# A hybrid decoder layer in split fp32: head products in runs of matmuls of one shape, activation rows at one byte remainder, block products pass by pass

## The chip, the cores and the metric

One core of one Trainium2 chip runs the whole layer as one program. The metric is the device time of an execution in microseconds; three executions of the kernel before gave 2039.51 to 2040.22, median 2040.07. TensorE (PE) multiplies, VectorE (DVE), ScalarE (ACT) and GpSimd (POOL) do the rest; SyncE (SP) and POOL issue the DMAs.

## The reference, cut to what matters

```python
h = concat([meta (16 rows), x (512 rows)])            # L = 528, D = 2048
p = rmsnorm(h, g_mix) @ w_in                          # q k v | b c u, 1024 columns each
q, k = rmsnorm per head of 128;  o_attn = stick_breaking_attention(q, k, v)   # 8 heads
o_conv = b * causal_dwconv3(c * u)
h = h + concat([rmsnorm(o_attn), rmsnorm(o_conv)]) @ w_out
n2 = rmsnorm(h, g_ffn)
h = h + (silu(n2 @ w_gate) * (n2 @ w_up)) @ w_down    # 5632 wide
return h[16:]
```

## The kernel before

Everything is kept transposed: channels on the 128 partitions, the 528 tokens on the free axis. The input x stands as 16 tiles of 128 channels (`nh0` to `nh15`), scaled by `g_mix`, each split into a rounded part `nh` and a remainder `nl` in the matmul type fp32r. A weight tile is split the same way into `hi` and `lo` in a ring `s_buf`: ACT casts `hi` (line 188), DVE subtracts for `lo` (line 189), `prepare` adds weight quarters where a Strassen product needs them (line 201). Each product is then three matmuls for each 128 x 128 weight block: `hi*ah`, `hi*al`, `lo*ah`. Weights come over SP's queue into `w_buf`.

The work runs in these stages, times from the profile: the eight heads and the first two channel blocks of the convolution (0 to 414 us), the Strassen pairs of the convolution (414 to 596), the output projection `po` (596 to 772), gate and up (772 to 1612), and down (to the end).

In the first stage `product_steps` takes one loaded weight piece of `m` blocks and goes block by block. `parts` says which columns of x go to which bank of PSUM. For k, v, c and u these are two parts, because one matmul writes at most one bank:

```python
product([(pk[:, 0, :H], 0, H), (pk[:, 1, :H], H, L)], n_hl)      # H = 264: two parts of 264
product([(pq[:, 0, :], META, L)], n_hl)                          # q: one part of 512
for j in range(m):
    for ps, a, b in parts: pe.matmul(ps, wh, ah[:, a:b], ...)    # L280
    for ps, a, b in parts: pe.matmul(ps, wh, al[:, a:b], ...)    # L282
    for ps, a, b in parts: pe.matmul(ps, wl, ah[:, a:b], ...)    # L284
    k += 1; tick()
```

So a k product is 16 blocks of six matmuls of 264 columns, whose moving operand alternates between the front and the back of a row and between `nh` and `nl`. A row of x is a tile of its own of 528 x 4 = 2112 bytes, that is 8 x 256 + 64, so neighbouring tiles begin at different remainders modulo 256. `tick()` counts blocks and starts the attention's steps (`after(n, work)`) in between; a list scheduler of the framework then orders each engine's instructions by priority and its own costs.

From channel block 2 on, the convolution and all of gate, up and down are Strassen pairs: `pair_product` makes two output blocks from seven block products `block_product(ps, act, ...)` into three PSUM banks `y`, `z`, `x`. Each has eight weight blocks, and the order is block by block: `hi*act0` (L742), `hi*act1` (L743), `lo*act0` (L744). Between them ACT copies a bank aside into `sides` (L768, L770, L772) and DVE combines (L774, L778, L783). In the convolution the two halves of x are 260 columns each; the sums of halves and quarters (`blk`) are formed by `form_blocks` during the heads, stored in DRAM (`fc`) and loaded back by POOL (L701, L708). In gate, up and down the operands have 256 columns, and their tiles (`slots`, `pad`) are laid out so that each block begins at the same remainder modulo 256; in `po` a row is 512 columns, 2048 bytes.

## Time and profile before

| What | Value |
|---|---|
| median of three executions | 2040.07 us |
| the profiled execution, its time | 2039.67 us |
| its span in the profile | 2038.0 us |
| PE busy, share of the span | 2028.5 us, 100% |
| DVE, ACT, POOL busy | 1718.7, 1049.0, 379.9 us |
| granted TensorE clock | 1.00 throughout |

A matmul's record lasts longer than its turn (a 256-column one 275 ns), since matmuls are pipelined. What a matmul costs the stream is the distance from its start to the next one's start, so that is read from the rows in order of time. Such a row reads: start, length, engine, line, operation, out<-in, rows * columns of the weights, partitions x columns of the moving operand, count. L numbers are lines of the kernel before.

### The profile page before, as it was taken

What the parts mean: (1) busy time and instruction counts of PE and PEld (TensorE: products, weight loads), DVE (VectorE), ACT (ScalarE), POOL (GpSimd) and SP (SyncE); (2) the same over time, 40 slices, a digit from 0 to 9 for tenths busy, and PEclk for the clock granted to TensorE, in tenths of its full rate; (3) what the DMA queues carried; (4) which work ended last, traced back from release to release, by engine and by line L of the source; (5) the groups of instructions that cost most, each with busy time, mean ns of one, the idle gap of its engine ahead of it and who ended that gap; (6) DMA issues with size and microseconds to landing.
All of it is one profiled execution on the core that took longest, in us unless ns stands there. A gap on an engine that the chain in (4) does not pass through costs nothing.

```text
span 2038.0 us, 39734 instructions
## 1 busy us (share of the span) xinstructions
PE 2028.5 (100%) x16158; PEld 1964.8 (96%) x16158; DVE 1718.7 (84%) x2202; ACT 1049.0 (51%) x1517; POOL 379.9 (19%) x532
## 2 busy tenths in 40 slices
PE   9999999999999999999999999999999999999999
PEld 8999999999998889999999999999999999999999
DVE  8788878588877678998988988988989988888887
ACT  7666666344443435554554554555555544444443
POOL 0111111210015440101111111110110252222111
PEclk9999999999999999999999999999999999999999
DMA  6333344753365656556555555555555999989864
GB/s 231 111 119 124 124 136 130 253 150 104 104 212 181 187 175 231 155 169 174 159 165 158 159 161 161 158 161 158 163 160 155 278 312 310 243 236 262 228 154 89
DMA packets 161863, 361.70 MB, mean 177 GB/s; under 512 B 13584, under 2 KB 73488, under 8 KB 161680
## 3 DMA queue, kind: packets, MB, share of 16 engines
q1 hardware_dynamic: 79744, 229.51, 35.5%
q0 software_dynamic: 81936, 129.65, 24.2%
q8 instruction: 127, 2.08, 0.4%
q14 instruction: 56, 0.46, 0.1%
HBM read 278.50 MB, written 80.61 MB: 176 GB/s over the span
## 4 chain that ended last, share of the span: by engine, by line
PE 93%; DVE 3%; ACT 2%; issue 1%; DMA 1%; POOL 0%; DVEq 0%; POOLq 0%; ACTq 0%
PE x L742 13%; PE x L744 13%; PE x L743 13%; PE z L742 6%; PE z L743 6%; PE z L744 6%; PE y L742 3%; PE y L743 3%; PE y L744 3%; PE po L843 3%; PE po L845 3%; PE po L844 3%; PE pv L280 2%; PE pv L284 1%; PE pv L282 1%
## 5 line engine op out<-in xcount | busy, mean ns | idle before, releaser
L188 ACT CAST s_buf<-w_buf 128x1024 fp32r<-128x1024 f32 (+2 forms) x665 | 659.3, 991 | 764.7 <-PE x L743 341.1
L189 DVE TENSOR_TENSOR s_buf<-w_buf,s_buf 128x1024 fp32r<-128x1024 f32 (+2 forms) x665 | 767.2, 1154 | 174.4 <-ACT s_buf L188 174.1
L742 PE MATMUL x<-f,s_buf 128*128 128x256 f32 x1408 | 387.7, 275 | 0.6 <-ACT sides L772 0.5
L744 PE MATMUL x<-f,s_buf 128*128 128x256 f32 x1408 | 387.2, 275 | 0.0
L743 PE MATMUL x<-f,s_buf 128*128 128x256 f32 x1408 | 387.2, 275 | 0.0
L201 DVE TENSOR_TENSOR w_buf<-w_buf 128x1024 f32<-128x1024 f32 (+1 forms) x243 | 277.5, 1142 | 14.7 <-DMA w_buf<-w_in 10.4
L742 PEld LDWEIGHTS x<-f,s_buf 128*128 128x128 f32 x1408 | 264.3, 188 | 1.4 <-ACT sides L772 0.9
L743 PEld LDWEIGHTS x<-f,s_buf 128*128 128x128 f32 x1408 | 264.3, 188 | 0.0
L744 PEld LDWEIGHTS x<-f,s_buf 128*128 128x128 f32 x1408 | 264.3, 188 | 0.0
L1038 POOL DMA_DIRECT2D fd<-s x147 | 103.6, 921 | 705.0 <-DVE s L295 703.7
L742 PE MATMUL z<-f,s_buf 128*128 128x256 f32 x704 | 193.6, 275 | 0.0
L743 PE MATMUL z<-f,s_buf 128*128 128x256 f32 x704 | 193.6, 275 | 0.0
L744 PE MATMUL z<-f,s_buf 128*128 128x256 f32 x704 | 193.6, 275 | 0.0
L744 PE MATMUL x<-ring,s_buf 128*128 128x256 f32 x608 | 167.3, 275 | 1.0 <-DVE s_buf L189 1.0
L742 PE MATMUL x<-ring,s_buf 128*128 128x256 f32 x608 | 167.2, 275 | 0.0
L743 PE MATMUL x<-ring,s_buf 128*128 128x256 f32 x608 | 167.2, 275 | 0.0
L742 PEld LDWEIGHTS z<-f,s_buf 128*128 128x128 f32 x704 | 132.1, 188 | 0.0
L744 PEld LDWEIGHTS z<-f,s_buf 128*128 128x128 f32 x704 | 132.1, 188 | 0.0
L743 PEld LDWEIGHTS z<-f,s_buf 128*128 128x128 f32 x704 | 132.1, 188 | 0.0
L1108 POOL DMA_DIRECT2D out_T<-d x62 | 60.2, 1001 | 302.7 <-DVE d L1116 232.3
L744 PEld LDWEIGHTS x<-ring,s_buf 128*128 128x128 f32 x608 | 114.1, 188 | 1.2 <-DVE s_buf L189 1.2
L742 PEld LDWEIGHTS x<-ring,s_buf 128*128 128x128 f32 x608 | 114.1, 188 | 0.0
(379 smaller groups left out, 5252.3 us busy)
## 6 DMA issues: line engine op xcount, KB each, us to landing
w_buf<-w_gu SPq DMA_DIRECT2D x176, 512.0 KB, 3.4
w_buf<-w_in SPq DMA_DIRECT2D x92, 512.0 KB, 3.4
fd<-s POOLq DMA_DIRECT2D x147, 256.0 KB, 5.2
w_buf<-w_down SPq DMA_DIRECT2D x96, 384.0 KB, 4.9
ring<-fd POOLq DMA_DIRECT2D x42, 768.0 KB, 8.7
w_buf<-w_out SPq DMA_DIRECT2D x32, 512.0 KB, 3.6
out_T<-d POOLq DMA_DIRECT2D x62, 256.0 KB, 5.4
fc<-st SPq DMA_DIRECT2D x8, 1040.0 KB, 6.2
```

The source lines that it names most:

```text
L188: sc.copy(hi, src)
L189: in_turn(ve.tensor_tensor(lo, src, hi.bitcast(F32), ALU.subtract), turn)
L201: in_turn(ve.tensor_tensor(sums[name], a, b, ALU.add), turn)
L280: pe.matmul(ps, wh, ah[:, a:b], start=k == 0, stop=False)
L742: pe.matmul(p, hi[:, kk], act(0, k), start=start and j == k == 0, stop=False, skip_group_check=skip)
L743: pe.matmul(p, hi[:, kk], act(1, k), start=False, stop=False, skip_group_check=skip)
L744: pe.matmul(p, lo[:, kk], act(0, k), start=False, stop=k == n - 1, skip_group_check=skip)
L843: pe.matmul(ps, hi[:, kk], ah, start=k == order[0], stop=False)
L844: pe.matmul(ps, hi[:, kk], al, start=False, stop=False)
L845: pe.matmul(ps, lo[:, kk], ah, start=False, stop=k == order[-1])
L1038: gp.dma_start(fd[c][s][:, :, k], t[:, :, i])
L1108: gp.dma_start(two(out[j]), c, accum_op=ALU.add)
```

## The change

- Rows of x: `nh` and `nl` of one channel tile become the two rows of one tile `n` with a pitch of 2304 bytes (9 x 256), from byte 48. All rows then begin at one remainder modulo 256.
- Heads and first convolution products: the row is cut at 272 (16 meta tokens and 256), so into 272 and 256 columns, q into 256 and 256; the two parts stand side by side in PSUM across the bank border, so later readers see one row of 528. The loop takes all blocks of a weight piece for the first part, then all for the second: 24 matmuls of one shape, then 24 of the other. `tick()` comes with the last part only.
- Convolution pairs: halves of 272 columns that overlap by 16, for c and u; the b product takes 256 of them. `blk` is laid out with a pitch of 1152 bytes.
- `block_product`: all `hi*act0`, then all `hi*act1`, then all `lo*act0`, everywhere.
- In `pair_product` the copies and combinations get the highest priority; in the first part of down the second sums are written behind the pair.
- x for `form_blocks` is loaded by a step of its own, earlier and in four DMAs of 272 columns; the scratch for POOL's DMA descriptors is 8192 bytes instead of 16384.

```diff
-            for j in range(m):
+            for i, ((ps, a, b), j) in enumerate((part, j) for part in parts for j in range(m)):
                 wh, wl = hi[:, j * P : (j + 1) * P], lo[:, j * P : (j + 1) * P]
-                ah, al = acts[k]
-                for ps, a, b in parts:
-                    pe.matmul(ps, wh, ah[:, a:b], start=k == 0, stop=False)
-                for ps, a, b in parts:
-                    pe.matmul(ps, wh, al[:, a:b], start=False, stop=False)
-                for ps, a, b in parts:
-                    pe.matmul(ps, wl, ah[:, a:b], start=False, stop=k == last)
-                k += 1
-                tick()
+                ah, al = acts[k + j]
+                pe.matmul(ps, wh, ah[:, a:b], start=k + j == 0, stop=False)
+                pe.matmul(ps, wh, al[:, a:b], start=False, stop=False)
+                pe.matmul(ps, wl, ah[:, a:b], start=False, stop=k + j == last)
+                if i % len(parts) == len(parts) - 1:
+                    tick()
+            k += m
...
-    H = L // 2
+    H, ROW = META + T2, 2304 // 4
...
-        nh = npool.tile([P, L], F32R, tag=f"nh{k}", name=f"nh{k}")
-        nl = npool.tile([P, L], F32R, tag=f"nl{k}", name=f"nl{k}")
+        n = npool.tile([P, 2 * ROW], F32R, tag=f"n{k}", name=f"n{k}")
+        n_row = n.rearrange("p (a t) -> p a t", a=2)[:, :, 12 : 12 + 2 * H]
+        nh, nl = (n_row[:, i, :L] for i in range(2))
...
+    def row_of(ps, a=0):
+
+        flat = ps.rearrange("p a b -> p (a b)")[:, 512 - H + a :]
+        return flat[:, : L - a], [(flat[:, : H - a], a, H), (flat[:, H - a : L - a], H, L)]
...
-    C0, CH = 8, (L - 8) // 2
+    CH = H
...
+        blk_x[k] = x4 = stage.tile([P, 4, CH], F32, tag="x4", name=f"x4_{k}")
+        for i, kk in ((0, k), (2, k + 8)):
+            for m in range(2):
+                nc.sync.dma_start(x4[:, i + m], xT[kk][:, m * T2 : m * T2 + CH])
...
-            product([(pk[:, 0, :H], 0, H), (pk[:, 1, :H], H, L)], n_hl)
+            product(row_of(pk)[1], n_hl)
...
-            product([(pq[:, 0, :], META, L)], n_hl)
+            product(row_of(pq, META)[1], n_hl)
...
+        if h:
+            after(22, lambda h=h: load_x4(h - 1))
...
-                    gp.dma_start(blk[:, i, part], fc[:, n, part], max_dma_last_dim=4160)
+                    gp.dma_start(blk[:, i, :, part, :CH], fc[:, n, part])
...
-        for j in range(m):
-            p, skip = ps[:, j * w : (j + 1) * w], m > 1 or not start
-            for k in range(n):
-                kk = slice((j * n + k) * P, (j * n + k + 1) * P)
-                pe.matmul(p, hi[:, kk], act(0, k), start=start and j == k == 0, stop=False, skip_group_check=skip)
-                pe.matmul(p, hi[:, kk], act(1, k), start=False, stop=False, skip_group_check=skip)
-                pe.matmul(p, lo[:, kk], act(0, k), start=False, stop=k == n - 1, skip_group_check=skip)
+        for wt, part in ((hi, 0), (hi, 1), (lo, 0)):
+            for j in range(m):
+                p, skip = ps[:, j * w : (j + 1) * w], m > 1 or not start
+                for k in range(n):
+                    kk = slice((j * n + k) * P, (j * n + k + 1) * P)
+                    first = start and wt is hi and part == j == k == 0
+                    pe.matmul(p, wt[:, kk], act(part, k), start=first, stop=wt is lo and k == n - 1, skip_group_check=skip)
...
         block_product(x, acts[2], False, m)
-        sc.copy(u2, x)
+        with tc.high_priority(1 << 20):
+            sc.copy(u2, x)
...
-        gbs = pair(conv_acts)
+        gbs = pair([last_of(act) for act in conv_acts], T2)
...
-            (lambda: load_acts(1, 6)) if j == KT // 4 - 1 else None, lambda: second_sums(4 * j, c2, 2),
+            (lambda: load_acts(1, 6)) if j == KT // 4 - 1 else None,
         )
+        second_sums(4 * j, c2, 2)
...
-    nc = bacc.Bacc("TRN2", target_bir_lowering=False, num_devices=1)
+    nc = bacc.Bacc("TRN2", target_bir_lowering=False, num_devices=1, dynamic_dma_scratch_size=8192)
```

What this does to the order of instructions is shown at three places. The first is PE at the start of the k product of head 3. `pk` is its PSUM tile, `nh`, `nl` and `n` with their numbers are tiles of x, `s_buf` the split weights. Before:

```order
L280 MATMUL pk_1569<-nh_170,s_buf 128x264 x2
L282 MATMUL pk_1569<-nl_171,s_buf 128x264 x2
L284 MATMUL pk_1569<-nh_170,s_buf 128x264 x2
L280 MATMUL pk_1569<-nh_174,s_buf 128x264 x2
L282 MATMUL pk_1569<-nl_175,s_buf 128x264 x2
L284 MATMUL pk_1569<-nh_174,s_buf 128x264 x2
```

In the change, at the place in the same product where the first part ends and the second begins on PE:

```order
L282 MATMUL pk_1704<-n_248,s_buf 128x272
L283 MATMUL pk_1704<-n_248,s_buf 128x272
L284 MATMUL pk_1704<-n_248,s_buf 128x272
L282 MATMUL pk_1704<-n_251,s_buf 128x272
L283 MATMUL pk_1704<-n_251,s_buf 128x272
L284 MATMUL pk_1704<-n_251,s_buf 128x272
L282 MATMUL pk_1704<-n_170,s_buf 128x256
L283 MATMUL pk_1704<-n_170,s_buf 128x256
L284 MATMUL pk_1704<-n_170,s_buf 128x256
L282 MATMUL pk_1704<-n_173,s_buf 128x256
```

The pairs of equal matmuls on one x tile have gone; 24 of 272 columns stand ahead of 24 of 256.

The second place is PE at the start of down, where the pair with `x_17616` (after: `x_18105`) follows the one with `x_17401` (after: `x_17890`); `ring` and `first` are operand tiles. Before, the scheduler put three matmuls of the new pair into the last block of the old one:

```order
L742 MATMUL x_17401<-first_17365,s_buf 128x256
L742 MATMUL x_17616<-ring_7922,s_buf 128x256
L743 MATMUL x_17616<-ring_7922,s_buf 128x256
L744 MATMUL x_17616<-ring_7922,s_buf 128x256
L743 MATMUL x_17401<-first_17365,s_buf 128x256
```

And in the change, on the same engine:

```order
L767 MATMUL y_17888<-first_17851,s_buf 128x256 x24
L767 MATMUL x_17890<-first_17854,s_buf 128x256 x24
L767 MATMUL x_18105<-ring_8411,s_buf 128x256 x24
L767 MATMUL z_18104<-first_17839,s_buf 128x256 x24
L767 MATMUL x_18105<-first_17842,s_buf 128x256 x24
```

The new pair now begins behind the old one's last block, and its `lo` matmuls are the last 8 of 24.

The third place is ACT in the second pair of gate and up, around the last copy of bank `x` into `sides` (`gu` is the gate's input, whose silu needs a table load). Before:

```order
L770 COPY sides<-z_8219 128x256
L188 CAST s_buf<-w_buf 128x1024
L1047 ACT_TABLE_LOAD
L1047 ACTIVATE gu_7930<-gu_7930 128x512
L772 COPY sides<-x_8220 128x256
```

In the change, on the same engine:

```order
L795 COPY sides<-z_8708 128x256
L191 CAST s_buf<-w_buf 128x1024
L798 COPY sides<-x_8709 128x256
L1072 ACT_TABLE_LOAD
L1072 ACTIVATE gu_8419<-gu_8419 128x512
```

The copy has moved ahead of the table load and the silu.

98 lines of the change are left out of this document (55 added, 43 removed).

## The prediction

> **What bounds the kernel now.** I read the page first: its busy times and the chain that ended last.
>
> ```profile
> span 2038.0 us, 39734 instructions
> ...
> PE 2028.5 (100%) x16158; PEld 1964.8 (96%) x16158; DVE 1718.7 (84%) x2202; ACT 1049.0 (51%) x1517; POOL 379.9 (19%) x532
> ...
> PE 93%; DVE 3%; ACT 2%; issue 1%; DMA 1%; POOL 0%; DVEq 0%; POOLq 0%; ACTq 0%
> ```
>
> PE is busy for the whole span and holds 93% of the chain. So the time is the sum of the distances between matmul starts, plus the few places where PE waits. Next the stage table (stretch, length, busy time and count of PE, PEld, DVE, ACT, POOL, granted clock, DMA share, GB/s) and PE's waits:
>
> ```profile
> 414.00:596.00 182.00, 181.25 (x1508) 180.62 (x1507) 151.10 (x165) 86.63 (x116) 15.40 (x15) 1.00 0.38 119
> ...
> 772.50:1612.00 839.50, 838.91 (x7389) 837.98 (x7389) 758.73 (x848) 435.85 (x580) 115.85 (x164) 1.00 0.57 167
> ...
> PE x L744 <- DVE s_buf L189: 1.2, 2, 1.0
> ...
> PE x L742 <- ACT sides_c L772: 0.5, 2, 0.3
> PE x L742 <- ACT sides L772: 0.5, 2, 0.2
> ```
>
> The clock is 1.00 and the waits (us in total, times, longest) are small. What is left is the distance itself, which I took from the rows in order of time. Output projection (512 columns), q (512), v (264) and convolution pairs (260), first and last of a stretch without other work:
>
> ```profile
> 649.78 0.39 PE L844 MATMUL po<-oc,s_buf 128*128 128x512 f32 x1
> ...
> 651.37 0.39 PE L845 MATMUL po<-oc_end,s_buf 128*128 128x512 f32 x1
> ...
> 142.76 0.39 PE L280 MATMUL pq<-nh,s_buf 128*128 128x512 f32 x1
> ...
> 144.85 0.39 PE L280 MATMUL pq<-nh,s_buf 128*128 128x512 f32 x1
> ...
> 126.36 0.41 PE L280 MATMUL pv<-nh,s_buf 128*128 128x264 f32 x2
> ...
> 127.81 0.41 PE L280 MATMUL pv<-nh,s_buf 128*128 128x264 f32 x2
> ...
> 446.09 0.28 PE L742 MATMUL x<-nh,s_buf 128*128 128x260 f32 x1
> ...
> 447.52 0.28 PE L742 MATMUL x<-nh,s_buf 128*128 128x260 f32 x1
> ```
>
> Between these starts lie 7, 9, 12 and 12 matmuls: 227.1, 232.2, 120.8 and 119.2 ns each. Gate and up, 256 columns, in 100 us:
>
> ```profile
> 1000.00:1100.00 100.00, 100.00 (x885) 1.00 0.55 161
> ```
>
> A record lasts 275 ns, so about two of the 885 began before the window: 100 us over 883 is 113.25 ns, 0.4424 ns a column. At that rate 512 columns take 226.5 (po does), 264 take 116.8 and 260 take 115.0. So q pays 5.7 ns too much for each matmul, k and v 4.0, the convolution 4.2. What sets po, gate, up and down apart in the code: shape and byte remainder stay the same from one matmul to the next. In q the shape is the same too and only the remainder changes, so the remainder alone is enough to cost.
>
> How long does a stream need to get back to its rate? After a wait, and at the change of shape from po to gate and up:
>
> ```profile
> 823.76 0.39 PE L742 MATMUL x<-f,s_buf 128*128 128x256 f32 x1 [0.25 <-ACT sides L772]
> 823.99 0.28 PE L743 MATMUL x<-f,s_buf 128*128 128x256 f32 x1
> ...
> 824.81 0.28 PE L744 MATMUL x<-f,s_buf 128*128 128x256 f32 x1
> ...
> 772.55 0.28 PE L742 MATMUL y<-f,s_buf 128*128 128x256 f32 x1
> ...
> 773.61 0.28 PE L742 MATMUL y<-f,s_buf 128*128 128x256 f32 x1
> ...
> 596.59 0.39 PE L843 MATMUL po<-oc,s_buf 128*128 128x512 f32 x1
> ...
> 597.73 0.39 PE L845 MATMUL po<-oc,s_buf 128*128 128x512 f32 x1
> ```
>
> From 823.99 seven matmuls take 0.82 us where the settled rate gives 0.793, nine take 1.06 instead of 1.019; the first five of po take 1.14 instead of 1.133. A break costs 0.03 to 0.04 us at 256 columns, spread over seven to nine matmuls, and next to nothing at 512.
>
> **The change part by part.** *Rows and runs.* Counts follow from the loops and agree with the groups by shape:
>
> ```profile
> L280 PE MATMUL pk<-nh,s_buf 128*128 128x264 f32 x256 | 52.9, 288 | 0.0
> ...
> L284 PE MATMUL pq<-nh,s_buf 128*128 128x512 f32 x128 | 50.7, 396 | 0.0
> ```
>
> Six such groups for k and v: 1536 of 264 columns at 120.8 ns, 185.5 us. Three for q: 384 at 232.2, 89.2 us. The first two channel blocks have 384 of 260 (119.2: 45.8 us) and 96 of 512 (22.3 us). Nine pairs of 7 x 24: 1512 of 260, 180.2 us; the stage table's 182.00 us with its waits agrees. Sum 523.0 us.
>
> After: k, v, c, u have half their matmuls at 272 and half at 256; q and b have two of 256 for one of 512; six pairs have 272 columns and three 256. That is 768 + 192 + 1008 = 1968 of 272 columns and 768 + 192 + 768 + 192 + 504 = 2424 of 256. At 0.4424 ns a column, 120.3 and 113.25 ns: 236.8 + 274.5 = 511.3 us, 11.7 less. No row shows a run of 272 columns; 120.3 takes it that 272 settles as 256 and 512 do. The bounds are the settled rate below and the unsettled surcharge of 4.0 to 4.2 ns above; I take the settled one, since it is the nearest in kind (one shape, one remainder).
>
> But the runs are short. In the order that was built I count 234 places where shape or remainder changes in these products: every part, every attention step between, and in `blk` each pass, since its second row lies 1152 bytes (4.5 x 256) behind the first. At 0.035 us: 8.2 us. Bounds: nothing (as at the start of po), or no settling at all (the first rival). I take 0.035, because that is what 256 columns show. Net: 523.0 to 519.5, **-3.5 us**.
>
> *Pass by pass.* In gate, up and down shape and remainder are one already, so the rate stays. What changes is when `lo` is needed. The long wait stands on the chain at the start of down, with one of its kind in the convolution:
>
> ```profile
> 1629.72 1.23 DVE s_buf L189
> ...
> 1631.00 0.39 PE x L744
> ...
> 430.66 1.15 DVE s_buf L189
> ...
> 431.85 0.39 PE x L744
> ```
>
> The waits' row has 1.2 us idle for the two. To the stream each costs more: a record runs 0.16 us past its turn, and the first matmul after a wait takes 0.23 us to the next instead of 0.11 (823.76 to 823.99). So 1.2 + 2 x 0.16 + 2 x 0.11 = 1.7 us. Behind 16 `hi` matmuls (1.8 us) instead of two, and with the new pair no longer put ahead of the old one's last block, both are covered: **-1.7 us**. Late next would be the sum for the following block (L201): DVE at 758.73 of 839.50 us has little to spare, so some may come back.
>
> *Priorities.* The copy behind the silu's table load held PE once, for 0.25 us idle and so 0.5 us of the stream:
>
> ```profile
> 801.88 1.28 ACT L1047
> ...
> 803.72 0.36 ACT sides L772
> ...
> 804.12 0.39 PE x L742
> ```
>
> The copy now stands ahead of it: **-0.5 us**. The two waits on `sides_c` keep the same cast ahead of the copy and stay. `second_sums` written later touches only c2 and its store, off PE's path: 0. ACT and DVE read one PSUM row of 528 columns for two of 264, and the convolution's taps take a few instructions more on DVE, which is idle 31 of 182 us there: 0.
>
> *Start.* The first pieces have two weight blocks each, and both x tiles are now wanted within the first part. PE already waits there for `nl`, 0.2 to 0.3 us at a time:
>
> ```profile
> 7.75 0.30 PEld L282 LDWEIGHTS pk<-nl,s_buf 128*128 128x128 f32 x2 [0.22 <-DVE nl L352]
> ```
>
> One more such wait: **+0.3**; none, or one in each of the five first pieces (1.3), are the bounds.
>
> *DMAs, hidden.* For each of the eight blocks of `form_blocks` SP issues four loads of x instead of two, and POOL loads `blk` in rows of 1088 bytes instead of 4160:
>
> ```profile
> 301.47 1.72 SPq L419 DMA_DIRECT2D x<-xT  x2
> ...
> 379.92 4.35 POOL L701 DMA_DIRECT2D blk<-fc  x6 [0.30 <-POOL acc_a L314]
> ...
> L742 PE MATMUL z<-blk,s_buf x16: 278/282/288, 419.8 to 428.0; 128*128 128x260 f32 x16
> ...
> DMA to landing us min/median/max: 5.8/13.1/20.9
> ```
>
> On SP that is 3.4 us instead of 1.7 ahead of the weight loads, which lead their use by two pieces (2 x 48 x 120.8 ns = 11.6 us): covered. On POOL four times the rows at, at worst, four times the 0.73 us makes 17 us of issue instead of 4.4; the last load (380 + 17 + 13 = 410) lands 10 us ahead of the first use. 0, and 5 us if the landing doubles. The smaller scratch binds only if these six queue up: in the same margin.
>
> Sum: -3.5 - 1.7 - 0.5 + 0.3 = **-5.4 us**. From the profiled execution's 2039.67 that is 2034.3; the median of the runs lies 0.4 higher, so **2034.7**.
>
> **The rivals.** *1, slower: the new runs don't settle and a matmul pays for columns and for being one.* In the stages in question every matmul pays about 4.1 ns on top of its columns, and there are 4392 instead of 3912. Then 511.3 + 18.0 = 529.3, +6.3 us, less the 2.0 of waits: 2044.4. For it speaks that attention steps cut the runs; against it that 256 and 512 settle elsewhere. It decides from 11.7 us / 4392 = 2.7 ns left on each matmul (3.1 with the waits). The Trainium skill ("TensorE: Matmul & The Clock Gate", Back-to-back issue gap) has a rule of this kind, columns / 2.4 plus 2.5 ns for each matmul, whatever stood before it. By it two of 264 equal 272 and 256, the extra 480 matmuls cost 1.2 us and the convolution's wider halves some 5, an estimate of +6 us in all; its 109 ns for 256 columns is not what the rows here show (113.25), nor is one price for q and po.
>
> *2, no change: 256 settles, 272 does not.* 272 columns are 1088 bytes, 4.25 x 256, so a row doesn't end where it began, unlike all that settles above. Then 1968 x 4.1 = 8.1 us and half of the breaks, 4.1: 523.5, +0.5, less 2.0: 2038.5.
>
> *3, faster: a change of shape on aligned rows costs next to nothing*, as at the start of po. Then breaks cost 2 us instead of 8: 2028.5.
>
> *4, POOL's or SP's loads come late*, as worked out above: 2034.7 + 5 = 2040.
>
> **How the numbers follow.** Forecast 0.46, rival 1 0.14, rival 2 0.20, rival 3 0.15, rival 4 0.05. The forecast's own range is 2031.5 to 2037.5 (breaks at 0.025 to 0.045 us, waits gone or half back). Over all cases 2028 to 2044 leaves out about 2 in 10: half of rivals 1 and 3 and some of the tails. The three runs before lie within 0.04%; I take 0.2%, 4.1 us, as what a measurement here tells from no change, so faster is under 2036.0 and slower over 2044.1. Faster: 0.85 of the forecast and rival 3, 0.54; slower: most of rival 1 and tails, 0.15; the same: 0.31.
>
> **What would show it.** Distances of 113.3 ns in the later two thirds of a run of 256 and about 120.3 in one of 272 show the rate right; 124 in all of a 272 run shows rival 2, and 117 in 256 runs rival 1. Runs that are settled from their second matmul show rival 3. PE's row of waits for `s_buf` from DVE should be gone. Gate and up should keep their 113.25. It would be wrong if the stage from 414 us did not get shorter, or if `blk` appeared among PE's waits.

## The result, and the profile after

The changed kernel is slower: 2052.80 us, median of four executions (2052.15 to 2056.86), against 2040.14 for the kernel before on the same chip. The ratio is 1.0065, 95% interval 1.0052 to 1.0077. The prediction was 2034.7, with a range of 2028 to 2044.

The page of the changed kernel: span, busy times, and the chain that ended last.

```profile
span 2055.1 us, 40757 instructions
...
PE 2033.9 (99%) x16638; PEld 1990.7 (97%) x16638; DVE 1721.6 (84%) x2210; ACT 1053.3 (51%) x1521; POOL 383.5 (19%) x532
...
PE 56%; DMA 2%; issue 1%; DVE 0%; POOL 0%; ACT 0%; POOLq 0%; DVEq 0%
```

PE is still busy nearly all the time, for 5 us more than before, but its share of the span is no longer 100%, and the chain, whose shares now add up to some 60% of the span only, has a transfer in it. Next the table by stage (stretch, length, busy time and count of PE, PEld, DVE, ACT, POOL, granted clock, DMA share, GB/s). First the changed kernel, in order the first products, the heads, the first two channel blocks, the convolution pairs, `po`, gate and up, down:

```profile
0.00:33.50 33.50, 29.96 (x212) 28.22 (x212) 26.78 (x44) 27.68 (x47) 1.09 (x8) 0.95 0.85 304
33.50:349.00 315.50, 307.73 (x2430) 299.26 (x2431) 247.40 (x421) 200.26 (x328) 49.15 (x105) 1.00 0.35 116
349.00:425.50 76.50, 75.45 (x621) 74.33 (x620) 46.07 (x68) 35.59 (x58) 20.84 (x37) 1.00 0.85 231
425.50:610.00 184.50, 184.50 (x1514) 184.37 (x1513) 158.03 (x175) 88.00 (x117) 20.26 (x18) 1.00 0.37 122
610.00:785.50 175.50, 175.17 (x777) 144.80 (x776) 123.88 (x165) 70.80 (x113) 76.52 (x82) 1.00 0.65 205
785.50:1625.00 839.50, 838.65 (x7390) 838.02 (x7389) 756.97 (x848) 435.61 (x580) 115.71 (x164) 1.00 0.56 167
1625.00:2055.10 430.10, 422.47 (x3705) 421.70 (x3704) 362.49 (x493) 195.37 (x281) 99.94 (x121) 1.00 0.87 232
```

The same cuts of the kernel before, for the four stages that changed by more than 1 us:

```profile
0.00:29.50 29.50, 28.36 (x164) 24.96 (x164) 24.14 (x40) 25.93 (x44) 1.09 (x8) 1.00 0.93 342
29.50:337.50 308.00, 307.28 (x2100) 285.54 (x2099) 253.29 (x426) 199.35 (x331) 48.95 (x106) 1.00 0.36 118
...
413.50:596.00 182.50, 181.75 (x1510) 181.00 (x1510) 151.10 (x165) 86.63 (x116) 15.40 (x15) 1.00 0.38 120
...
1612.00:2038.00 426.00, 420.65 (x3704) 419.89 (x3702) 360.88 (x494) 195.31 (x281) 101.65 (x120) 1.00 0.87 234
```

Start +4.0 us, heads +7.5, convolution pairs +2.0, down +4.1; the other three together -0.5. The four losses have different causes, so each is shown by its own rows. The profiled execution took 2056.86 us and is the slowest of the four (the others 2052.15 to 2053.08), so its start and its down are not typical: two short stretches at a lower clock, shown below, are in it. The heads took 314.3 to 315.9 us and the pairs 184.5 or 184.6 in all kernels below that leave both as changed.

**Heads.** PE's waits in the heads, changed kernel, then before (us in total, times, longest):

```profile
PE c L600 <- DVE spl L296: 5.2, 6, 1.0
...
PE c L588 <- DVE spl L295: 0.3, 1, 0.3
```

The attention of head h runs between the products of head h+1. Its last sum `c` needs a carried row: an earlier `c` on PE, `lw` on DVE, `sph` on ACT, `spl` on DVE. The rows of DVE for one head (the third), and PE's matmul that uses the result, in the changed kernel:

```profile
157.87 0.56 DVE L605 TENSOR_TENSOR lw<-c,sp 1x400 f32<-1x400 f32 x1
158.35 0.69 DVE L304 TENSOR_TENSOR tmp<-tmp 128x528 f32<-128x528 f32 x1
...
158.97 0.55 DVE L608 TENSOR_TENSOR lb<-lb,c 128x400 f32<-128x400 f32 x1
159.45 0.69 DVE L305 TENSOR_TENSOR tmp<-tmp,tmp 128x528 f32<-128x528 f32 x1
...
160.07 0.67 DVE L296 TENSOR_TENSOR spl<-lw,sph 1x512 fp32r<-1x512 f32 x1
...
160.79 0.50 PE L600 MATMUL c<-spl,carry 128*128 128x512 f32 x1 [0.98 <-DVE spl L296]
```

Two steps of the next head's reciprocal root (L304, L305) lie between `lw` and `spl`. Before, only `lb` and one short step did, and `spl` was there in time:

```profile
153.42 0.55 DVE L593 TENSOR_TENSOR lw<-c,sp 1x400 f32<-1x400 f32 x1
...
154.72 0.68 DVE L295 TENSOR_TENSOR spl<-lw,sph 1x512 fp32r<-1x512 f32 x1
...
155.58 0.39 PE L588 MATMUL c<-spl,carry 128*128 128x512 f32 x1
```

From `lw` to `spl` it is 1.30 us before and 2.20 after. This order goes back to the steps just ahead of `lw`. In the second head, up to these steps, DVE and ACT run within 0.1 us of each other in the two kernels, counted from the head's first `z` on PE. Then, before, a weight subtraction (`s_buf`) stands between the two halves of `tmp<-ss_k`, with which the reciprocal root begins. After, both halves stand ahead of it:

```profile
109.40 0.43 DVE L467 SCALAR_TENSOR_TENSOR tmp<-ss_k,acc_x 128x264 f32<-128x264 f32 x1
109.99 1.22 DVE L189 TENSOR_TENSOR s_buf<-w_buf,s_buf 128x1024 fp32r<-128x1024 f32 x1 [0.17 <-ACT s_buf L188]
111.13 0.42 DVE L467 SCALAR_TENSOR_TENSOR tmp<-ss_k,acc_x 128x264 f32<-128x264 f32 x1
...
112.96 0.77 DVE L478 SCALAR_TENSOR_TENSOR tmp<-ss_k,acc_x 128x272 f32<-128x272 f32 x2
113.64 1.22 DVE L192 TENSOR_TENSOR s_buf<-w_buf,s_buf 128x1024 fp32r<-128x1024 f32 x1
```

So ACT begins the root 1.01 us ahead of `lw` instead of 0.12 us behind it, and two of its steps on DVE are ready in time to be put ahead of `spl`. It is the same in the second to the seventh head: the root came early, and that made `spl` late. In the second head ACT does not wait for x, and PE waits 0.29 us for `spl`.

From the third to the seventh head PE waits 0.98 or 0.99 us. There the chain is also late already when it gets to these steps: ACT's scaling of x for `form_blocks` stands ahead of the casts of `sph` and waits for its load. The waits' row of the changed kernel, and that of before:

```profile
ACT x L436 <- DMA x<-xT: 10.6, 7, 2.2
...
ACT x L421 <- DMA x<-xT: 2.8, 6, 0.6
```

**Convolution.** Starts of whole block products, 24 matmuls each, 272 columns and then 256:

```profile
450.31 3.16 PE L767 MATMUL z<-blk,s_buf 128*128 128x272 f32 x24
453.31 3.17 PE L767 MATMUL x<-blk,s_buf 128*128 128x272 f32 x24
...
471.05 2.96 PE L767 MATMUL z<-blk,s_buf 128*128 128x256 f32 x24
473.84 1.44 PE L767 MATMUL x<-blk,s_buf 128*128 128x256 f32 x11
```

3.00 us are 125.0 ns for a matmul of 272 columns (120.3 was forecast); 2.79 us are 116.3 ns for 256, with the two changes of pass inside (24 x 113.25 ns would be 2.72).

**Start and down.** PE's waits in the first 30 us, and those in down:

```profile
PE pk L282 <- ACT n L354: 1.5, 3, 0.7
...
PE pk L283 <- DVE n L355: 0.6, 2, 0.4
...
PE y L767 <- DMA ring<-fd: 2.5, 2, 1.3
PE x L767 <- DMA ring<-fd: 1.3, 1, 1.3
```

The wait for `s_buf` at the start of down (1.0 us) is gone, and longer ones for the loads of the next operands have come: 3.8 us here, 2.1 to 2.5 us in the eight other kernels that also have `second_sums` behind the pair. In this execution both places are followed by 3.4 us at a clock of 0.50. The first row is from the start, where the 0.80 is the mean over 8 us; the others, 1 us each, are the place in down:

```profile
8.00:16.00 8.00, 7.90 (x50) 7.37 (x50) 7.02 (x12) 7.03 (x13) 0.00 (x0) 0.80 1.04 394
...
1716.00:1717.00 1.00, 0.21 (x2) 0.00 (x1) 0.87 (x1) 0.00 (x0) 0.71 (x2) 1.00 1.19 281
...
1719.00:1720.00 1.00, 1.00 (x7) 1.00 (x6) 0.00 (x0) 0.76 (x1) 0.23 (x1) 0.50 1.25 199
```

At a clock of 0.50, 7 matmuls are done in a us instead of 9.

### The profile page after: what moved, and what is told of

The parts are those of the page before. It is cut to its first block, busy times and chain, and to the rows that moved or that the text cites. A ratio compares the mean times of both kernels' runs of the same rounds, so it can differ in the third digit from the quotient of the medians.

```text
span 2055.1 us, 40757 instructions
## 1 busy us (share of the span) xinstructions
PE 2033.9 (99%) x16638; PEld 1990.7 (97%) x16638; DVE 1721.6 (84%) x2210; ACT 1053.3 (51%) x1521; POOL 383.5 (19%) x532
## 4 chain that ended last, share of the span: by engine, by line
PE 56%; DMA 2%; issue 1%; DVE 0%; POOL 0%; ACT 0%; POOLq 0%; DVEq 0%
PE x L767 32%; PE z L767 16%; PE y L767 8%; DMA ring<-fd 1%; DMA out_T<-d 1%; DVE s_buf L192 0%; POOL ring L1101 0%; POOL ring L1094 0%; POOL out_T L1133 0%; ACT s_buf L191 0%; DVE w_buf L204 0%; DVE d L806 0%; DVE d L1141 0%; DVE d L811 0%; DVE d L1195 0%
## 5 line engine op out<-in xcount | busy, mean ns | idle before, releaser
L767 PE MATMUL x<-f,s_buf 128*128 128x256 f32 x4224 | 500.7, 275 | 0.9 <-ACT sides L798 0.7
L767 PEld LDWEIGHTS x<-f,s_buf 128*128 128x128 f32 x4224 | 488.9, 188 | 1.4 <-ACT sides L798 0.9
L767 PE MATMUL z<-f,s_buf 128*128 128x256 f32 x2112 | 253.6, 275 | 0.0
L767 PEld LDWEIGHTS z<-f,s_buf 128*128 128x128 f32 x2112 | 245.9, 188 | 0.0
L767 PE MATMUL x<-ring,s_buf 128*128 128x256 f32 x1824 | 220.3, 276 | 1.3 <-DMA ring<-fd 1.3
L767 PE MATMUL y<-f,s_buf 128*128 128x256 f32 x1056 | 126.8, 275 | 0.0
L767 PEld LDWEIGHTS y<-f,s_buf 128*128 128x128 f32 x1056 | 123.1, 188 | 0.1
L767 PE MATMUL z<-ring,s_buf 128*128 128x256 f32 x864 | 105.7, 275 | 0.0
L767 PEld LDWEIGHTS z<-ring,s_buf 128*128 128x128 f32 x864 | 101.5, 188 | 0.0
L282 PE MATMUL pk<-n,s_buf 128*128 128x272 f32 (+1 forms) x256 | 73.7, 288 | 1.5 <-ACT n L354 1.5
L283 PE MATMUL pk<-n,s_buf 128*128 128x272 f32 (+1 forms) x256 | 73.1, 286 | 0.6 <-DVE n L355 0.6
L284 PE MATMUL pk<-n,s_buf 128*128 128x272 f32 (+1 forms) x256 | 72.7, 284 | 0.0
```

Source lines behind the costliest of these rows:

```text
L282: pe.matmul(ps, wh, ah[:, a:b], start=k + j == 0, stop=False)
L283: pe.matmul(ps, wh, al[:, a:b], start=False, stop=False)
L284: pe.matmul(ps, wl, ah[:, a:b], start=False, stop=k + j == last)
L767: pe.matmul(p, wt[:, kk], act(part, k), start=first, stop=wt is lo and k == n - 1, skip_group_check=skip)
```

## The experiments

Each kernel was timed several times against the kernel before on the same chip (2040.05 to 2040.43 us in all of them), but for `widths`, which was executed once. A ratio's interval is some 2.5 us wide to either side for most kernels, so two versions that differ by 1 or 2 us can't be told apart by their medians; there the rows of the stages and waits carry the reading. For comparison by stage I use the profiled execution of each, from the first matmul of one stage to the first of the next (us):

| kernel | start | heads | 2 blocks | pairs | po | gate, up | down | median us | ratio, 95% interval |
|---|---|---|---|---|---|---|---|---|---|
| before | 24.6 | 307.9 | 76.1 | 182.6 | 176.0 | 840.2 | 421.4 | 2040.14 | 1 |
| changed | 28.2 | 315.9 | 76.4 | 184.5 | 175.2 | 839.9 | 425.4 | 2052.80 | 1.0065, 1.0052 to 1.0077 |
| passes_only | 24.4 | 308.1 | 76.1 | 181.7 | 175.2 | 839.7 | 422.8 | 2039.46 | 0.9998, 0.9989 to 1.0007 |
| rows_only | 26.6 | 314.9 | 76.5 | 184.6 | 175.9 | 840.2 | 420.6 | 2052.26 | 1.0058, 1.0046 to 1.0070 |
| after_k9 | 27.7 | 313.4 | 76.7 | 184.5 | 175.2 | 839.7 | 423.8 | 2050.23 | 1.0051, 1.0039 to 1.0063 |
| after_start | 24.9 | 314.3 | 76.5 | 184.5 | 175.2 | 840.0 | 424.0 | 2051.43 | 1.0058, 1.0046 to 1.0070 |
| after_sums_in | 26.4 | 314.5 | 76.6 | 184.6 | 175.2 | 839.9 | 422.5 | 2051.69 | 1.0058, 1.0044 to 1.0072 |
| after_mend | 25.8 | 313.2 | 76.7 | 184.5 | 175.2 | 839.7 | 422.3 | 2048.03 | 1.0038, 1.0026 to 1.0051 |
| best2 | 24.4 | 307.9 | 76.2 | 181.7 | 175.2 | 839.7 | 423.0 | 2039.45 | 0.9995, 0.9987 to 1.0004 |
| after_gap | 27.0 | 314.6 | 76.9 | 184.5 | 175.2 | 839.7 | 422.5 | 2051.43 | 1.0054, 1.0042 to 1.0067 |
| after_mend3 | 25.4 | 314.3 | 77.0 | 184.5 | 175.2 | 839.7 | 422.3 | 2049.55 | 1.0048, 1.0034 to 1.0062 |
| before_k7 | 25.3 | 311.1 | 75.9 | 182.6 | 176.0 | 840.2 | 420.9 | 2042.83 | 1.0012, 1.0003 to 1.0021 |
| after_blocks | 25.0 | 310.3 | 76.3 | 184.5 | 175.2 | 840.0 | 421.8 | 2045.73 | 1.0028, 1.0018 to 1.0039 |
| after_x2 | 27.0 | 316.0 | 76.9 | 184.5 | 175.2 | 839.7 | 421.8 | 2054.94 | 1.0068, 1.0055 to 1.0081 |
| before_x4 | 24.2 | 307.9 | 76.7 | 182.6 | 176.0 | 840.2 | 420.6 | 2040.38 | 1.0003, 0.9994 to 1.0012 |
| after_260 | 28.3 | 315.1 | 76.7 | 179.6 | 175.2 | 839.7 | 422.0 | 2048.38 | 1.0038, 1.0024 to 1.0051 |
| mend_all | 25.6 | 317.3 | 76.8 | 180.0 | 175.2 | 839.9 | 422.3 | 2047.66 | 1.0035, 1.0023 to 1.0048 |
| after_xbuf | 28.6 | 314.5 | 74.8 | 194.0 | 175.8 | 839.7 | 421.9 | 2059.92 | 1.0100, 1.0083 to 1.0117 |
| mend_gate | 25.8 | 313.5 | 75.3 | 179.6 | 175.2 | 839.7 | 422.3 | 2042.53 | 1.0011, 1.0002 to 1.0020 |

Down runs to the last matmul's end, and some 9 to 11 us before the first and behind the last matmul belong to no stage. A stage is one execution's. The start (26.4 to 28.6 us in eight kernels that share it) and down (421.8 to 425.4 in the eight here that have `second_sums` behind the pair) also differ by whether the clock fell there in the execution that was profiled; a median of the whole is the stricter number.

### The two halves of the change

**passes_only**: the kernel before with the new `block_product` and the raised priorities, nothing else.

> The kernel before with only the pass-by-pass order in block_product and the five raised priorities (rows, widths, k/v/q order, second_sums and scratch as before). Theory A (the loss comes with the rows): the two waits for lo and the one behind the table load go as the prediction said, nothing else moves: 2040.1 - 2.2 = 2037.9 us, no wait for ring at the start of down. Rival B (pass by pass itself brings the late ring loads in down): about +4 us there, 2042.

**rows_only**: the changed kernel with those put back.

> The changed kernel with block_product, the priorities and second_sums put back as before: only rows, widths, the part-by-part order in q, k, v and the smaller scratch are left. Theory A: the heads lose 8 us to waits of the sums in the attention steps (c at its second matmul, some 1 us in each of heads 2 to 7), the start loses 3.5 us, the products in the heads gain 2 and the convolution loses 2 (272 columns not settled), the two lo waits are back but no ring wait: 2040.1 + 8 + 3.5 = 2051 to 2052 us. Rival B (the loss comes with pass by pass and second_sums): the prediction's own -3.5 + 0.3, 2037 us.

2039.46 and 2052.26: all of the loss that medians can tell comes with rows and runs, as theory A has it, and pass by pass by itself can't be told from no change. Its gain of 0.9 us in the pairs, 0.8 in `po` and 0.5 in gate and up was partly given back in down, where PE now waits for the copy of `x` instead of the `lo` part. PE's row in down, `passes_only`:

```profile
PE x L744 <- ACT sides L769: 2.8, 3, 1.3
```

**best2** keeps the old order in down's first four pairs:

```diff
+        if m > 1:
+            for j in range(m): ...        # block by block, as before
+            return
         for wt, part in ((hi, 0), (hi, 1), (lo, 0)):
...
-        with tc.high_priority(1 << 20):
+        with tc.high_priority(1 << 20) if m == 1 else ExitStack():
```

> The kernel before with pass by pass and the raised priorities for the convolution, gate and up only; the blocks of down with two weights columns (its first four pairs) keep the old order and priorities. Theory A (in down the order of passes moved the wait from lo to the copy of x, 1.4 us worse; elsewhere it gains 0.5 to 1 us): 2038 to 2039 us, down 421 us. Rival B: no difference from before, 2040 us.

2039.45, but down took 423.0, not 421: PE waited for another step of ACT there (`z` for `d`, 1.4 us once). Theory A was wrong on down; the total is no different from `passes_only`.

**after_sums_in** puts `second_sums` back inside the pair.

> The changed kernel with second_sums back inside the pair, ahead of the pair's last blocks. Theory A (the late ring loads at the start of down come from writing second_sums, and with it its marker for the next loads, behind the last block): no wait for ring, but the copies of x wait for DVE as in the run with pass by pass alone (2.8 us idle, 3 times): down takes 422 to 423 us instead of 425, 2052.8 - 2 = 2050.5 us. Rival B (the smaller scratch or the rows delay the loads): the ring waits stay, 2052 to 2053 us.

The ring waits are gone. Down took 422.5 us, against 425.4 in the changed kernel's profiled execution but 421.8 to 424.0 in the other kernels with the sums behind, so no gain is shown. In place of the ring came the copies, as in `passes_only`:

```profile
PE x L767 <- ACT sides L792: 2.5, 3, 1.0
```

So in down one wait was traded for another each time: `lo` (before), the copies (sums inside), the loads (sums behind).

### The start

**after_start**: the pieces of head 0 that run while x arrives go block by block.

```diff
-            for i, ((ps, a, b), j) in enumerate((part, j) for part in parts for j in range(m)):
+            pairs_of = [(part, j) for part in parts for j in range(m)]
+            if early: pairs_of.sort(key=lambda p: p[1])
+            for i, ((ps, a, b), j) in enumerate(pairs_of):
```

> The changed kernel with the first products of head 0 (the pieces that run while x is still arriving) in the old order, block by block, in all else as changed. Theory A (PE waits for n of the second x tile and then runs some 5 us at half clock): the first products end 3 to 3.5 us sooner, at about 24 us after the start as before; 2052.8 - 3.3 = 2049.5 us. Rival B (the x tiles and weights arrive when they arrive, later blocks wait instead): 2052 to 2053 us.

The start is back at 24.9 us and the waits for `n` are gone; theory A's mechanism holds. The whole gained 1.4 us, not 3.3: part of the 3.6 us lost at the start of the changed kernel's profiled execution was the 3.4 us at half clock. Kernels with the same start took 28.2 to 28.6 us where the clock fell and 26.4 to 27.7 where it did not.

### The heads

**after_k9** lets in the step that finishes k one block later; on DVE only `lb` then stands between `lw` and `spl`.

```diff
-        after(8 if h else 11, qk_norm(row_of(pk)[0], g_k, ...))
+        after(9 if h else 11, qk_norm(row_of(pk)[0], g_k, ...))
```

> The changed kernel with one number changed: the step that finishes k of a head is let in 9 block steps after its product and not 8. On DVE the three reciprocal-root steps then stand behind the correction of row 0 of spl and no longer between lw and spl. Theory A (c waits because DVE makes spl after two steps of the next head's rsqrt): the waits c <- spl (5.2 us idle, about 6 us of the stream) are gone, 2052.8 - 6 = 2047 us. Rival B (c waits on the chain of c, lw, sph, spl itself, whatever stands between): c keeps waiting, 2052 to 2053 us.

-2.6 us of the 6 expected. The wait for `spl` fell, but one for `sph` came up (heads only):

```profile
PE c L599 <- ACT sph L295: 1.4, 3, 0.5
PE c L600 <- DVE spl L296: 1.4, 7, 0.2
```

**before_k7** does the opposite in the kernel before: 7 instead of 8, so that two of the reciprocal-root steps stand between `lw` and `spl`.

> The kernel before with one number changed: the step that finishes k of a head comes 7 block steps after its product and not 8. On DVE two of the reciprocal-root steps of the next head then stand between lw and spl, as they do in the changed kernel; rows, widths and runs stay as before. Theory A (the order of DVE's steps around spl alone costs the wait): c <- spl some 0.7 to 1 us in each of six heads, 2045 to 2046 us. Rival B (it needs the new rows and runs as well): 2040 us.

2042.83, ratio 1.0012 (1.0003 to 1.0021), between the two theories: the heads took 3.2 us more. From `lw` to `spl` it is 1.93 us there. PE's row for the whole run (2.3 of the 2.6 us and 7 of the 8 times are in the heads):

```profile
PE c L588 <- DVE spl L295: 2.6, 8, 0.4
```

So an order on DVE alone costs something there, with rows and runs as before, but less than half of the 8.0 us that the changed kernel's heads lose.

**after_mend** joins `after_k9`, `after_start` and `after_sums_in`; **after_gap** and **after_mend3** add one block step between the last two sums:

```diff
-                after(6, lambda: sums(s - 1))
+                after(6 if s == 2 else 7, lambda: sums(s - 1))
...
-                after(11, lambda: mix(ws))
+                after(10, lambda: mix(ws))
```

> The changed kernel with three mends together: k finished one block step later, the first pieces of head 0 block by block, second_sums back inside. Theory A (three separate losses, which add): -2.6 (k), -3.3 in the first 28 us, -2 in down: 2052.8 - 8 = 2045 us, and what is left over before (some 5 us) lies in the heads (waits behind the attention steps) and in the convolution (+2). Rival B (what PE gains early it waits for later, since the weight loads of the heads set the pace): 2049 to 2050 us.

> The run with k finished one block step later (2050.2 us), and in it the last sum of a head, sums(0), let in 7 block steps after sums(1) and not 6; mix follows 10 and not 11 steps later, so that it stays where it was. Theory A (c waits because its chain c, lw, sph, spl no longer fits into six block steps): the remaining waits of c in the heads (2.8 us idle, some 4 us of the stream) go, 2046 to 2047 us. Rival B (ACT and DVE are behind as a whole, and the next step waits instead): 2049 to 2050 us.

> The same longer distance in the run with the three mends (2048.0 us). Theory A: 2044 us, and all that is left over before are 2 us in the convolution, 1 us in the start and 1 us in down. Rival B: 2047 to 2048 us.

2048.03, 2051.43 and 2049.55. The three mends gave 4.8 us together, between the two theories. More room for `c` gave nothing: now `z` waits for DVE's copy of `v` (1.8 us in the heads of `after_mend3`, 4 times), and the heads stay at 314 us, as rival B has it.

**after_blocks** is the changed kernel with q, k, v, c, u and b block by block again:

```diff
-            for i, ((ps, a, b), j) in enumerate((part, j) for part in parts for j in range(m)):
+            for i, ((ps, a, b), j) in enumerate((part, j) for j in range(m) for part in parts):
```

> The changed kernel with q, k, v, c, u and b block by block again (three matmuls of 272 columns, then three of 256), rows and all else as changed: what the longer runs are worth. Theory A (in runs of 24 the surcharge is 3.0 ns for k, v, c, u and 1.3 for q and b, in runs of three it is 4.1 for all): the products cost 4 to 5 us more, the first pieces give 3.3 back: 2053 to 2054 us. Rival B (a change of shape on aligned rows costs next to nothing): 2049 to 2050 us. The waits c <- spl stay by both, since DVE's order there is the same.

2045.73, 7 us less than the changed kernel, and outside both theories. The products pay about the surcharge theory A named (4.4 ns a matmul above 0.4424 ns a column in k and v instead of 3.3, from the distances between starts), yet the heads took 310.3 us instead of 315.9. DVE's order between `lw` and `spl` is the same as in the changed kernel, and PE waits there three times instead of six:

```profile
PE c L600 <- DVE spl L296: 2.0, 3, 1.0
```

From the second to the seventh head, counted from each head's first `z`, the last cast of `sph` from `sp` on ACT is 0.8 to 1.8 us later in the changed kernel than in this one. From the third head on ACT's scaling of x differs by only -0.1 to 0.6 us, so the load of x does not explain it. The rows show another difference, in all six heads. In the changed kernel, as in the one before, DVE does a weight subtraction (`s_buf`) ahead of `lb`, and a step of POOL on `sp` that runs beside it lasts 1.20 us; here `lb` comes first, and the same step lasts 0.28. In the changed kernel and then in this one, third head:

```profile
149.29 1.20 POOL L557 TENSOR_SCALAR_AFFINE_SELECT sp<-sp 128x112 f32<-128x112 f32 x1 [1.21 <-DVE sp L569]
...
145.24 0.28 POOL L557 TENSOR_SCALAR_AFFINE_SELECT sp<-sp 128x112 f32<-128x112 f32 x1 [1.21 <-DVE sp L569]
```

ACT's cast of `sph` waits for that step, 1.1 to 1.3 us there and 0.2 to 0.3 here. So at least 0.9 us a head of what the order of the products costs comes through the order of DVE's steps. By these rows the kernel before has the long step but an early x, and 1.30 us from `lw` to `spl`; this one has a late x and 2.20 us but the short step; the changed kernel has all three delays.

**after_x2** and **before_x4** test whether the four loads of x instead of two are what makes ACT late.

```diff
-            for m in range(2):
-                nc.sync.dma_start(x4[:, i + m], xT[kk][:, m * T2 : m * T2 + CH])
+            src = bass.AP(row.tensor, row.offset, [row.ap[0], [T2, 2], [1, CH]])   # row = xT[kk]
+            nc.sync.dma_start(x4[:, i : i + 2], src)
```

> The changed kernel with the x rows of form_blocks loaded by two transfers a block (each with both overlapping halves of 272 columns) and not four. Theory A (four loads are issued one behind the other on SP's queue, 4.0 us and not 1.3; the last lands late, ACT's scaling of x waits for it 10.6 us in all, and sph, spl and c stand behind that): ACT waits for x some 3 us as before, the waits of c for spl (5.2 us idle) mostly go, 2046 to 2047 us. Rival B (DVE's order around spl alone makes c wait): 2052 us.

> The kernel before with the x rows of form_blocks loaded by four transfers a block and not two, in all else as before. Theory A (the late x alone delays the attention's casts): ACT waits for x 7 to 10 us instead of 2.8 and PE waits for spl in most heads, 2043 to 2046 us. Rival B: the chain before has room for it, 2040 us.

Both fell out for rival B: 2054.94 and 2040.38. With two loads ACT waits as long:

```profile
ACT x L438 <- DMA x<-xT: 11.1, 6, 2.4
```

The number of loads is not the cause. They start late, some 1.3 us after the head's first `z` instead of 0.7, although their step stands earlier in the program: `x` has one buffer, which the step `st` on DVE frees, and `st` is itself some 0.6 us later against `z` than in the kernel before.

**after_xbuf** gives x a second buffer (and takes 2 KB of the scratch).

> The changed kernel with a second buffer for the x rows of form_blocks (and 2 KB less of scratch to make room), so that they are loaded a head earlier; the orders on DVE and ACT around spl stay. Theory A (a ring of waits from head to head, st - store - x loads - scaling on ACT - sph - spl - c - next head's st, is longer than PE's work for a head): ACT's waits for x (10.6 us) vanish, c <- spl falls from 5.2 us to under 2, 2046 to 2048 us. Rival B (only the order around spl counts): 2052 us.

It didn't test what it was meant to. The scheduler moved the scaling forward with the loads, so that ACT still waited (7.7 us, 6 times), and in the convolution one copy was late by a whole stretch, which costs the pairs 9.5 us:

```profile
PE x L767 <- ACT sides_c L792: 6.4, 1, 6.4
```

**mend_all** joins `after_x2`, `after_start`, `after_sums_in` and the 260 columns of the next part. **mend_gate** adds a dependence, so that the scaling can't be placed ahead of the casts:

```diff
+        gx, g2 = stage.tile([P, 2], F32, ...), g_mix[:, k : k + 9 : 8]
+        ve.scalar_tensor_tensor(gx, bhs[-1][:, :2].bitcast(F32), 0.0, g2, ALU.mult, ALU.add)
...
-            sc.activation(x4[:, i : i + 2], x4[:, i : i + 2], AF.Copy, scale=g_mix[:, kk : kk + 1])
+            sc.activation(x4[:, i : i + 2], x4[:, i : i + 2], AF.Copy, scale=gx[:, i // 2 : i // 2 + 1])
```

> The changed kernel with four mends together: two x loads a block, the first pieces of head 0 block by block, second_sums back inside, and 260 columns in the convolution's wide pairs. Theory A (the causes are apart and add: -6, -3.3, -1, -5.5): 2037 us, at or below the kernel before. Rival B (ACT and DVE are behind in the heads anyway): 2042 us or more.

> The run with four mends (2047.7 us), and in it the factor that scales the x rows of form_blocks is made (one 128x2 step on DVE) only after bh, so that on ACT the scaling stands behind the casts of sph and sh_k and not ahead of them; on DVE only lb then stands between lw and spl. Theory A (the ring of waits through the x loads and ACT is what makes c wait in the heads): ACT no longer waits for x, c <- spl falls from 5.4 us idle to under 1.5, 2038 to 2040 us. Rival B (ACT and DVE have too much to do between two heads' products, whatever their order): c or the next step keeps waiting, 2046 to 2048 us.

2047.66 (rival B: in its heads `c` waits as in the changed kernel), then 2042.53: the dependence gave 5.1 us, 3.8 of it in the heads and 1.5 in the two blocks behind them, and ACT no longer waits for x at all. It moved two things, though: ACT's scaling behind the casts, and DVE's two root steps from ahead of `spl` to behind it (from `lw` to `spl` 1.30 us again), so how much each gave is not shown. Theory A named the place, but of its 8 to 10 us only 5 came. `c` still waits, because `st` (1.28 us) now stands on DVE ahead of `lw`. PE's row in the heads:

```profile
PE c L607 <- ACT sph L298: 3.7, 6, 0.9
```

### Which widths settle

**after_260**: the wide pairs of the convolution compute only the last 260 of their 272 columns, which are all that the taps read; 260 as before, now at one remainder.

```diff
+        acts = [lambda part, k, act=act: act(part, k)[:, cut:] for act in acts]      # cut = 12
-        x = pair_product(acts, two(c1), two(c2), sides)
+        x = pair_product(acts, two(c1)[:, :, cut:], two(c2)[:, :, cut:], sides)
```

> The changed kernel with the halves of the convolution's wide pairs cut from 272 columns to the last 260, which are all that the taps read: 260 columns as before, but now at one remainder. Theory A (the prediction's premise: one shape at one remainder settles at 0.4424 ns a column): 115 to 117 ns a matmul instead of 125.0, 1008 of them, -8 to -10 us: 2043 to 2045 us. Rival B (what is no multiple of 256 columns pays some 4.5 ns at one remainder too): 119.5 ns, -5.5 us, 2047 us.

**widths** cuts five of the six wide pairs to other widths; its result leaves out the columns cut.

> One look at distances in the convolution's pairs: the halves of five of the six wide pairs are cut from 272 columns to 264, 240, 224, 208 and 192 (the columns cut are left out of the result). Theory A (one shape and one remainder are enough, as the prediction had it; 272 should then have run at 120.3 ns): 116.8, 106.2, 99.1, 92.0, 84.9 ns. Theory B (only multiples of 256 columns settle, all else pays some 4.5 ns): 121.3, 110.7, 103.6, 96.5, 89.4. Theory C (a run settles on whole steps of 6.67 ns, of which 256 columns take 17, whenever its columns fill them nearly): 240 in 16 steps, 106.7; 224 in 15, 100.0; 208 in 14, 93.3; 192 in 13, 86.7; 264 and 272 fall between and stay at 120 to 121 and 125 to 127.

`after_260` took 2048.38 us, 4.4 less than the changed kernel; its pairs 179.6 instead of 184.5. Block products of 260 columns (`after_260`), then of 264 and of 240 and 192 (`widths`):

```profile
425.88 3.05 PE L767 MATMUL y<-n,s_buf 128*128 128x260 f32 x24
428.76 3.04 PE L767 MATMUL x<-n,s_buf 128*128 128x260 f32 x24
```

```profile
449.52 3.07 PE L767 MATMUL z<-blk,s_buf 128*128 128x264 f32 x24
452.43 3.07 PE L767 MATMUL x<-blk,s_buf 128*128 128x264 f32 x24
...
489.12 2.85 PE L767 MATMUL z<-blk,s_buf 128*128 128x240 f32 x24
...
580.59 2.84 PE L767 MATMUL z<-blk,s_buf 128*128 128x192 f32 x24
```

260 columns take 2.88 / 24 = 120.0 ns, not the 115.0 of the forecast's premise; 264 take 121.3. By these numbers theory B (a surcharge of some 4.5 ns: 119.5 and 121.3) and theory C (120.0, and 120 to 121) both hold. The single distances, which the merged rows leave out, speak against whole steps of 6.67 ns: of 966 distances of 260 columns 701 are 120 ns, which is 18 steps, but 272 columns settle on a cycle of 124, 126, 127 and 123 ns. So 260, 264 and 272 do settle, each at a rate of its own (0.462, 0.459 and 0.460 ns a column against 0.4424); what sets these rates is not shown.

Nor do 256 columns always settle at 113.3. In the three pairs of the changed kernel that have them, the blocks on `n` whose operand begins at the first half of a row or 1024 bytes (4 x 256) behind it do (2.72 us for 24, once settled). The block on the sums stored in `n`, 1088 bytes (4.25 x 256) behind it, keeps one shape and one remainder too, and takes 2.85 us, 118.8 ns, all three times. In the `blk` block from 471.05 the first eight distances are at 113.3 and the 16 behind the change of pass at 117.9 on average.

Below 256 no theory held: 240 and 192 columns take nearly the same (2.85 and 2.84 us with records of 0.27 us, so 2.58 / 23 = 112 ns). There something else than the columns sets the distance, and whether those widths fill steps can't be seen. The Trainium skill ("TensorE: Matmul & The Clock Gate", Back-to-back issue gap) says that the load of the weights and the matmul together set the distance in a stream, and that its columns / 2.4 plus 2.5 ns, which the prediction applied to the stream, is the distance of an isolated matmul. The first would fit this row, with some 112 ns as the least for a new 128 x 128 block each time; no run here has the load of the weights alone.

## Why the prediction was wrong, point by point

Two steps failed. The larger is a term that was put at nothing: what ACT and DVE do with one row of 528 columns, where the heads lost 8.0 us, above all to waits of PE for `spl` (5.2 of 7.6 us idle; the last point below). The other is the rate of the new runs, which came out at about nothing instead of -3.5. None of the four rivals had the heads.

- **Rate of the new runs (-3.5).** Its step "one shape, one remainder" as enough to settle at 0.4424 ns a column is what failed. 272 took 125.0 ns instead of 120.3: 4.7 us in the pairs alone, of which 1.9 show as a loss against before since three pairs became narrower. This is rival 2's mechanism (272 does not settle at that rate) and near its price (4.1 ns). That the stage from 414 us gets no shorter had been named as a sign of error, and it came: 182.6 to 184.5. And 256 columns settled only at some remainders, above. In the heads the surcharge above 0.4424 ns a column did shrink, from 4.0 to 3.3 ns a matmul in k and v and from 4.0 for 512 columns to twice 1.4 in q: with c, u and b some 2.6 us less in all, from the distances between starts. With 1.9 us more in the pairs and an estimated 0.7 for the eight columns more of each row of c and u (192 x 8 x 0.4424 ns) the term comes to about nothing. For q the prediction had 5.7, from nine matmuls; the mean of 337 distances is 230.5 ns and not 232.2.
- **Breaks at 0.035 us.** A `blk` block of 256 columns took 2.79 to 2.81 us, 0.07 to 0.09 more than a settled one. For the two or three breaks counted there that is about the term's size, but not its mechanism: the run did not get back to its rate within seven to nine matmuls, it stayed at 117.9 ns to the end. Rival 1 had named that (no settling at all), for all runs.
- **Pass by pass (-1.7).** Both waits for `lo` went, as said. What would be late next was named wrongly: not the sum L201, but ACT's copies in down or, with `second_sums` behind the pair, the loads of `ring`. Net -0.7 us (`passes_only`), within what can be told.
- **Priorities (-0.5).** Gate and up went from 840.2 us to 839.7 to 840.0 in all kernels that have them, which is about the size. No run has the priorities without the new order of passes, and in the changed kernel the two waits for the copy of `x` (0.5 us) went but one of 0.7 us for the same copy came in a later pair.
- **Start (+0.3, bounds 0 to 1.3).** 3.6 us in the profiled execution, 1.8 to 4.0 in the other kernels with the same start. The bound counted one DVE wait a piece. Missing were PE's waits for ACT's part of `n` (1.5 us in three waits) and the clock, 0.50 for 3.4 us.
- **DMAs, hidden (0).** Right for SP's four loads (`before_x4`, 2040.38) and for `blk`, which is in no wait of PE. Late loads came in other places than rival 4 had them: `ring` at the start of down, and x in the heads, for which ACT waits 10.6 us instead of 2.8.
- **The heads, which the sum left out.** The largest loss, 8.0 us, stands against a term of 0: "ACT and DVE read one PSUM row of 528 columns for two of 264". It looked at DVE's idle time in the convolution and not at the carried row in the heads, where before `spl` ended only 0.18 us ahead of PE's matmul (155.40 to 155.58). The profile before showed that margin. From `lw` to `spl` 0.90 us were added, and from the third head on `lw` itself came 0.5 to 1.4 us later against `z`.

What is shown of the heads: the loss comes with rows and runs (`rows_only`); most of it goes with the part-by-part order (`after_blocks`, -5.6 us in the heads); DVE's order between `lw` and `spl` alone is worth about 3 us (`before_k7`); that order and ACT's wait for x ahead of `sph` together are worth 5 (`mend_gate` against `mend_all`). The rows show which came first: the reciprocal root moved ahead of a weight subtraction in the second head, where x is not waited for. What is not shown: why the scheduler chose that order with the new rows and runs, and how the 8.0 us divide between that order, the late x and POOL's longer step. That the delays feed each other from head to head (`spl`, `c`, the split of w, q's root, `st`, the x load, ACT, `sph`, `spl`) fits the rows, but the one run meant to open that ring without moving other steps, `after_xbuf`, didn't open it. The description of the change ahead of the prediction has one error: `tick()` is called at every second group of three matmuls and so stays spread evenly over a piece; it does not come with the last part only.

No version is measurably faster than the kernel before; `best2` and `passes_only` come nearest with 0.9995 and 0.9998.

## What to carry to other kernels

A stream that is bound by PE still hangs on chains through DVE and ACT that end just in time: read the margin of each (here 0.18 us for `spl`) before counting an edit there at nothing, since a scheduler that reorders by its own costs can spend it. A wait that is taken away at one place shows its worth only when the next late thing is known; in down three versions each had another one. Before a layout is built on a rate, run the very width: 256 columns settling did not mean that 272 or 260 would, nor that 256 would at another byte remainder.

## What the runs showed of the hardware

- In settled runs of one shape and one remainder a matmul took 113.3 ns with 256 columns, 120.0 with 260, 121.3 with 264 and 125.0 with 272; a run of 256 columns whose operand begins 4.25 x 256 bytes further took 118.8.
- A fresh 128 x 128 weight block each time took about 112 ns however narrow the matmul was, from 240 down to 192 columns.
- A step of POOL (128 x 112) took 0.28 us beside one step of DVE (`lb`) and 1.20 us beside another (the weight subtraction), in six heads out of six each; ACT's wait for it differed by as much.
- Some 1.5 us of work in 4 us was enough for the clock to fall to 0.50 for 3.4 us (down, 1714 to 1721), though no single wait was over 1.3 us; in `after_260`, with two waits of 2.2 us together at that place, it did not fall. The Trainium skill ("TensorE: Matmul & The Clock Gate", Part 1: The HAM clock gate) says that the state follows how busy the PE was over a free-running window of some 3.4 us, and that the low state is half the clock; the 0.50 and the length agree.
